# Ones matmuls ahead of the first rows, squares behind each tile's split, and a later first load of down-projection weights, in a one-core two-layer encoder step

## The chip, the core and the metric

The kernel runs on one core of one Trainium2 chip. The metric is device microseconds (us) of the whole program; a lower time is better. The kernel before took 1649.12 us, the median of three runs (1648.03 to 1649.99 us). A profiled execution of it was recorded too; all rows below come from that one.

## The reference, cut to what matters

One step of a streaming encoder with two layers, on 512 prompt rows and 32 sample rows of width 1024, in fp32. The start of the program, which the change touches, computes the first of these lines for layer 0:

```python
def rmsnorm(x, g):
    y = xf * lax.rsqrt(jnp.mean(xf * xf, axis=-1, keepdims=True) + EPS)
    return y * g
...
for l in range(DEPTH):                       # DEPTH = 2
    h = rmsnorm(x, w['norm_mix_g'])
    z = h @ w['w_in']                        # q, k, v, gmlp u and v: 1024 -> 2560
    ...                                      # differential attention, spatial gate, norms
    x = x + jnp.concatenate([o, g_out], -1) @ w['w_out']
    x = x + cross_attend(rmsnorm(x, w['norm_x_g']), mem_k, mem_v, wq_c, wo_c, xq_norm_g)
    g, up = jnp.split(rmsnorm(x, w['norm_ffn_g']) @ w['w_up'], 2, -1)   # 1024 -> 2 x 2816
    x = x + (silu(conv3(g)) * up) @ w['w_down']                         # 2816 -> 1024
```

Outputs are the rows after both layers and the new keys, values and convolution states.

## The kernel before, in words

Every large product is done with split operands: an fp32 tile is cut into a high part (a cast to fp32r by ScalarE, written ACT in the rows) and a low part (source minus high part, by VectorE, DVE), and three products (high by high, high by low, low by high) are summed in PSUM by TensorE (PE). Weights go through the same split: `emit_item` takes a loaded tile `raw` and makes the pair `hl` (L192 on ACT, L193 on DVE).

**Start (L1136 to L1186).** The gain row `mrow` and the 32 sample rows `xs` are loaded from ACT's queue. The first of four prompt tiles `xin` (128 rows by 1024, 512 KB each) is issued on SyncE's queue (SP); then `prefetch(4)` lets `load` issue weight loads, then the other three prompt tiles follow on the same queue. PE transposes each prompt tile in two halves of four 128 by 128 blocks (`pxin`, L1174) and the sample rows by 16 thin matmuls (`pxis`, L1179). `take` follows each: DVE multiplies by the gain into `xg` (L1162), ACT casts the high part into `hx` (L1163) and copies the plain rows into `x` (L1164), DVE makes the low part (L1165). After the loop over tiles, ACT squares the five row tiles (L1184), summing each row into one column of `sx`, from which `x_stats` makes the reciprocal roots (`rsq`), their diagonal matrices `dg` and the broadcast `rbc`. Since the mean is applied after the product, the first projection (`pr`, L370 to L372, 128 by 256 outputs) needs `hx` and `hl` and not the squares.

**Weight loads.** `load` keeps two tiles of kind "raw" (512 KB) and two of kind "rawb" (halves of a down-projection block, 384 KB) in flight. A tile is issued as soon as the tile two places ahead of it in its kind has been split. `items` is the list of all splits in order of use, `state["emitted"]` how many have been written out. The first "rawb" pair is used by item 74 in layer 0 and by item 266 in layer 1; in the kernel before it is issued at item 0, and at items 185 and 188.

**Order.** The instructions of each engine and queue run in the order in which a planner put them when the program was built: it walks the program with estimated durations and takes, among what it holds to be ready, the instruction that comes first in the text. So a change of the text can change the order of instructions in other places too.

Of the kernel before, what the change touches and what calls it, by code (L numbers as in the profile page):

```python
# [12 lines left out]
AF = mybir.ActivationFunctionType  # L13
ALU = mybir.AluOpType
# [5 lines left out]
SS = 32  # L20
# [16 lines left out]
def encoder_step(ctx: ExitStack, tc: tile.TileContext, a, o):  # L37
    nc = tc.nc
    vec, act, pool, pe, sp = nc.vector, nc.scalar, nc.gpsimd, nc.tensor, nc.sync
# [7 lines left out]
    def psR(name):  # L47
        return pp.tile([128, 512], F32, tag="R", bufs=4, name=name)

    def psS(name):  # L50
        return pp.tile([128, 512], F32, tag="S", bufs=2, name=name)
# [6 lines left out]
    def G(tag, shape, name, dt=F32):  # L58
        return gp.tile(shape, dt, tag=tag, bufs=GB[tag], name=name)

    def tmp(shape, name, tag="t", bufs=5, dt=F32):
        return tp.tile(shape, dt, tag=tag, bufs=bufs, name=name)

    ONCE = ("sx", "vx", "ve", "rx", "dgs", "ssm", "vm", "gss", "mss", "sss", "ls")

    def tiny(shape, name, dt=F32):
        return tp.tile(shape, dt, tag="y_" + name, bufs=1 if name in ONCE else 2, name=name)

# [6 lines left out]
    ones = cp.tile([128, 128], F32, name="ones")  # L75
# [10 lines left out]
    raws, items = [], []  # L86
# [4 lines left out]
    for i in range(NP):  # L91
        q = i // PART - 1
        n = min(PART, NP - PART * (q + 1)) * 4 - 1
        for b in range(4):
            PLAN.append(("gguu"[b], i, b % 2))
            p = 4 * (i - PART * (q + 1)) + b - 1
# [3 lines left out]
    def build_units():  # L100
        def ks(src, k0, n):
            return src[k0 * 128:(k0 + n) * 128].rearrange("(k p) c -> p k c", p=128)

        def item(tag, what, ids, n):
            items.append((tag, what, ids, n))
            for r in ids:
                raws[r][2] = len(items) - 1

        def raw(loads, nk, cols, kind="raw"):
            raws.append([loads, nk, None, cols, kind])  # L110
            return len(raws) - 1

        def two(tag, mat, cols):
            for k0 in (0, 4):
                c0, loads = 0, []
                for c, n in cols:
                    loads.append((0, 4, c0, n, ks(mat[:, c:c + n], k0, 4)))
                    c0 += n
                item(tag, None, (raw(loads, 4, 256),), 4)

        for l in range(DEPTH):
            wi = a["w_in"][l]
            kq = lambda h: two(f"kq{h}", wi, [(512 + 128 * h, 128), (128 * h, 128)])
            v_ = lambda j: two(f"v{j}", wi, [(1024 + 256 * j, 256)])
            u_ = lambda j: two(f"u{j}", wi, [(1536 + 256 * j, 256)])
            gv = lambda j: two(f"gv{j}", wi, [(2048 + 256 * j, 256)])
            for f, i in ((kq, 0), (v_, 0), (kq, 1), (kq, 2), (v_, 1), (kq, 3), (gv, 0), (u_, 0), (gv, 1), (u_, 1)):
                f(i)
            for j in range(4):
                src = a["w_out"][l][:, 256 * j:256 * j + 256].rearrange("(b q k p) c -> q b p k c", b=2, q=2, p=128)  # L130
                for q in range(2):
                    item(f"wout{j}", None, (raw([(2 * b, 2, 0, 256, src[q, b]) for b in range(2)], 4, 256),), 4)
            for h in range(4):
                for nm in ("wq", "wk") if h == 0 else ("wk", "wq"):
                    two(f"{nm}{h}", a[nm + "_c"][l], [(256 * h, 256)])
                two(f"wv{h}", a["wv_c"][l], [(256 * h, 256)])
            for j in range(4):
                two(f"wo{j}", a["wo_c"][l], [(256 * j, 256)])

            ids = None  # L140
            for what, i, j in PLAN:
                if what != "d":
                    c0 = 256 * i + 128 * j + (FF if what == "u" else 0)
                    item(f"{what}{i}_{j}", None, (raw([(0, 8, 0, 128, ks(a["w_up"][l][:, c0:c0 + 128], 0, 8))], 8, 128),), 8)
                    continue
                jj, m = j // 7, j % 7
                if m == 0:
                    src = a["w_down"][l][256 * PART * i:256 * PART * (i + 1), 256 * jj:256 * jj + 256].rearrange(
                        "(k e p) c -> e p k c", e=2, p=128)
                    ids = [raw([(0, PART, 0, 256, src[e])], PART, 256, "rawb") for e in range(2)]  # L150
                item(f"d{i}_{jj}", SEVEN[m], ids, PART)
                raws[ids[0]][2] = min(raws[ids[0]][2], len(items) - 1 - max(0, m - 3))
            for j in range(4):
                n = NF - 2 * PART * NB
                item(f"dp{j}", None, (raw([(0, n, 0, 256, ks(a["w_down"][l][:, 256 * j:256 * j + 256], NF - n, n))], n, 256),), n)
# [4 lines left out]
    state = {"emitted": 0, "popped": 0, "held": 0}  # L160
    SLOTS = 8
    RAWS = {"raw": 2, "rawb": 2}
    waiting, loaded = {}, {}

    def load():
        if not waiting:
            for kind in RAWS:
                waiting[kind] = [r for r in range(len(raws)) if raws[r][4] == kind]
                loaded[kind] = 0
        for kind, n in RAWS.items():  # L170
            while loaded[kind] < len(waiting[kind]):
                k = loaded[kind]
                if k >= n and raws[waiting[kind][k - n]][2] >= state["emitted"]:
                    break
                r = waiting[kind][k]
                loads, nk, _, cols, _ = raws[r]
                t = wp.tile([128, 1024 if kind == "raw" else 256 * PART], F32, tag=kind, bufs=n, name="raw")
                rv = t[:, 0:nk * cols].rearrange("p (k c) -> p k c", c=cols)
                for k0, kn, c0, cn, src in loads:
                    sp.dma_start(out=rv[:, k0:k0 + kn, c0:c0 + cn], in_=src)  # L180
                raw_t[r] = rv
                loaded[kind] += 1
# [39 lines left out]
    def prefetch(slots=SLOTS):  # L222
        while state["emitted"] < len(items) and state["held"] + cost(state["emitted"]) <= slots:
            state["held"] += cost(state["emitted"])
            emit_item()
# [76 lines left out]
    def psR2(name, n=0):  # L302
        f = psS if n % 3 == 2 else psR
        return [f(name + "a"), f(name + "b")]
# [832 lines left out]
    build_units()  # L1137
    mrow = tmp([8, 128], "mrow")
    act.dma_start(out=mrow, in_=a["norm_mix_g"][0].rearrange("(k p) -> k p", p=128))
    xs = G("zr", [128, 1024], "xins")  # L1140
    vec.memset(xs[32:64], 0.0)
    vec.memset(xs[64:128], 0.0)
    act.dma_start(out=xs[0:32], in_=a["x_sample"][0])
    xin = []
# [12 lines left out]
    def take(ps, k0, nk, t0, n):  # L1157

        ps = ps[:, 0:nk * n].rearrange("p (k t) -> p k t", k=nk)
        xg = tmp([128, 512], "xg")[:, 0:nk * n].rearrange("p (k t) -> p k t", k=nk)  # L1160
        h = [hx[:, k0:k0 + nk, j, t0:t0 + n] for j in range(2)]
        vec.tensor_tensor(out=xg, in0=ps, in1=gmix[:, k0:k0 + nk].unsqueeze(2).to_broadcast([128, nk, n]), op=ALU.mult)  # L1162
        act.copy(h[0], xg)  # L1163
        act.copy(x[:, k0:k0 + nk, t0:t0 + n], ps)  # L1164
        vec.tensor_tensor(out=h[1], in0=xg, in1=f32(h[0]), op=ALU.subtract)  # L1165

    sx = tiny([128, 5], "sx")
    pool.memset(sx, 1.0)
    for t in range(4):
        for hk in range(2):  # L1170
            ps = (psB if hk else psS)("pxin")
            for k in range(4):
                kt = 4 * hk + k
                pe.transpose(ps[:, 128 * k:128 * k + 128], xin[t][:, 128 * kt:128 * kt + 128], ident)  # L1174
            take(ps, 4 * hk, 4, 128 * t, 128)
        if t == 0:
            ps = psS("pxis")
            for kt in range(8):
                pe.matmul(out=ps[:, 32 * kt:32 * kt + 32], lhsT=xs[:, 128 * kt:128 * kt + 128], rhs=ident[:, 0:32],  # L1179
                          start=True, stop=True)  # L1180
            take(ps, 0, 8, S0, SS)
    for t, (v, n) in enumerate([(v, 128) for v in xin] + [(xs, SS)]):
        jk = G("t4", [128, 1024], "jk")
        act.activation(out=jk[0:n], in_=v[0:n], func=AF.Square, accum_out=sx[0:n, t:t + 1])  # L1184
    prefetch()
    sp.dma_start(out=rope, in_=a["rope"])  # L1186

# [1 line left out]
    for l in range(DEPTH):  # L1189
# [3 lines left out]
        r, ve, rbc = x_stats(True, sx if l == 0 else None)  # L1193
# [38 lines left out]
        for j in range(4):  # L1232
            w2 = pop(f"wout{j}")
            for i in range(2):
                ps = psR2("pwo", 2 * j + i + 2)
# [3 lines left out]
        mt, rm, vm = do_memT(l)  # L1239
        _, ve, _ = x_stats(False)  # L1240
        co = []
        for h in range(4):
# [7 lines left out]
            for dc in range(2):  # L1250
                t = G(COTAGS[2 * h + dc], [128, 2, T], "co", F32R)
                co.append(t)
            do_cross_out(l, h, mv, pT, pTs, co)
        for j in range(4):
            w2 = pop(f"wo{j}")
            for i in range(2):
                ps = psR2("pwc")
# [3 lines left out]
        _, _, rbc = x_stats(True)  # L1261
# [50 lines left out]
```

## Time and profile before

| | |
|---|---|
| median of three runs | 1649.12 us (1648.03 to 1649.99) |
| profiled execution, whole | 1648.65 us |
| its span, first to last instruction | 1646.6 us |
| PE busy | 1619.5 us, 98% of the span |
| DVE busy | 1149.7 us, 70% |
| ACT busy | 778.6 us, 47% |
| POOL (GpSimd) busy | 536.2 us, 33% |
| mean transfer rate over the span | 96 GB/s |

The span is what the profile shows; the execution is 2.05 us longer than it. Busy shares are means over the whole program. The start of the program, some 30 us, is told by the timelines below and not by these shares. In the timelines an x8 stands for eight instructions merged into one line, whose time is from the first's start to the last's end. A matmul with fp32 operands is two instructions; a transpose, and a matmul with fp32r operands, is one.

### The profile page before, as it was taken

The page shows a single profiled execution, that of the slowest core. Times are in us where ns is not written, and L with a number is a line of the kernel's source. Part 1 is how long each engine was busy: PE and PEld are TensorE (multiplying, and loading weights), DVE is VectorE, ACT ScalarE, POOL GpSimd, SP SyncE. Part 2 cuts the span into 40 slices and gives each one's busy share as a digit, 9 for nine tenths or more (in the row PEclk, how much of TensorE's full clock was granted, in tenths as well). Part 3 has the DMA queues.
Part 4 walks back from the last instruction along what each step waited for, and adds up shares of the span by engine and source line. Part 5 has one row for each costly group of instructions (what it writes and reads, how often), then busy time and mean ns, then how long its engine had stood idle before and what let it go on. Part 6 is the DMA issues. An engine that isn't in the chain of part 4 may idle for free.

```text
span 1646.6 us, 33007 instructions
## 1 busy us (share of the span) xinstructions
PE 1619.5 (98%) x12897; PEld 1591.7 (97%) x12897; DVE 1149.7 (70%) x2453; ACT 778.6 (47%) x1625; POOL 536.2 (33%) x910
## 2 busy tenths in 40 slices
PE   8999999999999999999999999999999999999998
PEld 8999999899999999999999999999999999999998
DVE  7778765655477777877768777655555777778774
ACT  6657744554344334343445685545543433343332
POOL 2110042222244654543321000422222545555440
PEclk9999999999999999999999999999999999999999
DMA  7322224332322332323342212243422323323322
GB/s 215 96 80 81 86 83 142 106 119 91 90 78 74 91 106 81 103 75 97 111 123 63 90 55 91 90 129 109 135 84 78 90 81 91 95 82 93 91 81 82
DMA packets 217633, 158.06 MB, mean 96 GB/s; under 512 B 8414, under 2 KB 216166, under 8 KB 217478
## 3 DMA queue, kind: packets, MB, share of 16 engines
q1 hardware_dynamic: 217414, 155.82, 31.2%
q8 instruction: 101, 1.65, 0.4%
q14 instruction: 54, 0.44, 0.1%
q10 hardware_dynamic: 64, 0.14, 0.0%
HBM read 144.83 MB, written 11.10 MB: 95 GB/s over the span
## 4 chain that ended last, share of the span: by engine, by line
PE 93%; DVE 2%; ACT 2%; POOL 2%; issue 1%; DMA 1%; ACTq 0%; SPq 0%; DVEq 0%; POOLq 0%
PE pfga L353 8%; PE pfgb L353 8%; PE pfua L353 8%; PE pfub L353 8%; PE p7a L1084 6%; PE pr L370 4%; PE pr L372 4%; PE pr L371 4%; PE p7c L1084 3%; PE pwoa L353 3%; PE pwca L353 3%; PE pqb L353 3%; PE pwob L353 3%; PE pqa L353 3%; PE pwcb L353 3%; PE pm L372 2%
## 5 line engine op out<-in xcount | busy, mean ns | idle before, releaser
L193 DVE TENSOR_TENSOR hl<-raw,hl 128x1024 fp32r<-128x1024 f32 x216 | 279.7, 1296 | 93.8 <-ACT hl L192 89.5
L192 ACT CAST hl<-raw 128x1024 fp32r<-128x1024 f32 x216 | 226.6, 1049 | 164.4 <-PE pm L371 37.5
L353 PE MATMUL pfga<-hx,hl 128*128 128x272 f32 x1056 | 264.5, 287 | 0.0
L353 PE MATMUL pfgb<-hx,hl 128*128 128x272 f32 x1056 | 264.4, 287 | 0.0
L353 PE MATMUL pfua<-hx,hl 128*128 128x272 f32 x1056 | 259.9, 288 | 3.0 <-DVE gb L1024 3.0
L353 PE MATMUL pfub<-hx,hl 128*128 128x272 f32 x1056 | 259.7, 287 | 0.0
L353 PEld LDWEIGHTS pfua<-hx,hl 128*128 128x128 f32 x1056 | 195.6, 188 | 3.2 <-DVE gb L1024 3.2
L353 PEld LDWEIGHTS pfga<-hx,hl 128*128 128x128 f32 x1056 | 198.5, 188 | 0.0
L353 PEld LDWEIGHTS pfgb<-hx,hl 128*128 128x128 f32 x1056 | 198.4, 188 | 0.0
L353 PEld LDWEIGHTS pfub<-hx,hl 128*128 128x128 f32 x1056 | 195.5, 188 | 0.0
L370 PE MATMUL pr<-hl,hx 128*128 128x256 f32 x512 | 145.6, 285 | 0.7 <-DVE zvs L413 0.7
L371 PE MATMUL pr<-hl,hx 128*128 128x256 f32 x512 | 146.0, 286 | 0.0
L372 PE MATMUL pr<-hl,hx 128*128 128x256 f32 x512 | 145.5, 285 | 0.0
L1084 PE MATMUL p7a<-at,hl 128*128 128x272 f32 x864 | 121.8, 287 | 0.0
L1084 PEld LDWEIGHTS p7a<-at,hl 128*128 128x128 f32 x864 | 113.3, 188 | 0.0
L210 ACT CAST hl<-S 128x384 fp32r<-128x384 f32 x96 | 48.4, 512 | 113.0 <-POOL S L200 40.9
L370 PEld LDWEIGHTS pr<-hl,hx 128*128 128x128 f32 x512 | 98.2, 192 | 1.4 <-DVE zvs L413 1.2
L372 PEld LDWEIGHTS pr<-hl,hx 128*128 128x128 f32 x512 | 97.0, 190 | 0.4
L371 PEld LDWEIGHTS pr<-hl,hx 128*128 128x128 f32 x512 | 97.1, 190 | 0.3
L210 ACT CAST hl<-raw 128x384 fp32r<-128x384 f32 x72 | 36.6, 511 | 108.3 <-PE pfub L353 60.9
L353 PE MATMUL pwca<-co,hl 128*128 128x272 f32 x384 | 87.5, 289 | 0.0
L353 PE MATMUL pwcb<-co,hl 128*128 128x272 f32 x384 | 87.1, 288 | 0.0
(393 smaller groups left out, 4201.6 us busy)
## 6 DMA issues: line engine op xcount, KB each, us to landing
raw<-in_w_up_dram SPq DMA_DIRECT2D x88, 512.0 KB
raw<-in_w_down_dram SPq DMA_DIRECT2D x48, 384.0 KB
raw<-in_w_in_dram SPq DMA_DIRECT2D x24, 512.0 KB
raw<-in_w_in_dram SPq DMA_DIRECT2D x32, 256.0 KB
raw<-in_w_out_dram SPq DMA_DIRECT2D x32, 256.0 KB
raw<-in_wq_c_dram SPq DMA_DIRECT2D x16, 512.0 KB
raw<-in_wk_c_dram SPq DMA_DIRECT2D x16, 512.0 KB
raw<-in_wv_c_dram SPq DMA_DIRECT2D x16, 512.0 KB
```

Source lines behind the costliest of these rows:

```text
L192: act.copy(hi, src)
L193: vec.tensor_tensor(out=lo, in0=src, in1=f32(hi), op=ALU.subtract)
L210: act.copy(hl[:, 0], src)
L353: pe.matmul(out=ps[0 if n0 == 0 else 1][:, 0:nn], lhsT=hl[wpart][:, kk, col * 128:col * 128 + 128], rhs=mv[:, n0:n0 + nn], start=first and ...
L370: pe.matmul(out=out, lhsT=lh(k), rhs=hl[0][:, k % 4], start=(k == 0), stop=False)
L371: pe.matmul(out=out, lhsT=lh(k), rhs=hl[1][:, k % 4], start=False, stop=False)
L372: pe.matmul(out=out, lhsT=ll(k), rhs=hl[0][:, k % 4], start=False, stop=(k == k8 - 1))
L1084: pe.matmul(out=ps, lhsT=w[:, wpart, k], rhs=mv[:, part], start=fresh and k == 0 and wpart + part == 0, stop=k == PART - 1 and wpart == 1, ...
```

## The change

Four edits. (1) Twenty matmuls of `ones` by `ones` (fp32, 128 columns) into a PSUM tile that nothing reads stand ahead of the loop over prompt tiles, and one Square of a column of `ones` on ACT ahead of them. (2) The squares of a row tile come right after that tile's two `take`s, in two halves of 512 columns, each summed into its own column of `sx2`; their unused elementwise result goes over `xg`, which `take` now returns. DVE adds the two columns into `sx`. The tile of 32 sample rows comes last. (3) A "rawb" tile is issued only when its first item is at most 8 items ahead of the item that is written out (`EARLY`). (4) So at the start the two first "rawb" tiles are no longer issued ahead of the prompt tiles 1 to 3, but at item 66; layer 1's first pair is issued at item 258.

```diff
-    ONCE = (..., "mss", "sss", "ls")
+    ONCE = (..., "mss", "sss", "ls", "sx2")
...
-            raws.append([loads, nk, None, cols, kind])
+            raws.append([loads, nk, None, cols, kind, len(items)])
...
+    EARLY = 8
...
-                loads, nk, _, cols, _ = raws[r]
+                loads, nk, _, cols, _, first = raws[r]
+                if kind == "rawb" and first > state["emitted"] + EARLY:
+                    break
...
+    dum = tmp([128, 1], "dum", tag="aTs", bufs=1)
+    act.activation(out=dum, in_=ones[:, 0:1], func=AF.Square)
+    pw = psR("pwarm")
+    for i in range(20):
+        pe.matmul(out=pw[:, 0:128], lhsT=ones, rhs=ones, start=True, stop=True)
     xs = G("zr", [128, 1024], "xins")
...
         vec.tensor_tensor(out=h[1], in0=xg, in1=f32(h[0]), op=ALU.subtract)
-
-    sx = tiny([128, 5], "sx")
-    pool.memset(sx, 1.0)
+        return xg.rearrange("p k t -> p (k t)")
+
+    sx2 = tiny([128, 5, 2], "sx2")
+    pool.memset(sx2, 0.5)
+    def squares(t, hk, n, v, junk):
+        act.activation(out=junk[0:n], in_=v[0:n, 512 * hk:512 * hk + 512], func=AF.Square,
+                       accum_out=sx2[0:n, t, hk:hk + 1])
+    junks = []
     for t in range(4):
         for hk in range(2):
...
-            take(ps, 4 * hk, 4, 128 * t, 128)
+            junks.append(take(ps, 4 * hk, 4, 128 * t, 128))
+        for hk in range(2):
+            squares(t, hk, 128, xin[t], junks[2 * t + hk])
         if t == 0:
...
-    for t, (v, n) in enumerate([(v, 128) for v in xin] + [(xs, SS)]):
-        jk = G("t4", [128, 1024], "jk")
-        act.activation(out=jk[0:n], in_=v[0:n], func=AF.Square, accum_out=sx[0:n, t:t + 1])
+    for hk in range(2):
+        squares(4, hk, SS, xs, junks[7])
+    sx = tiny([128, 5], "sx")
+    vec.tensor_tensor(out=sx, in0=sx2[:, :, 0], in1=sx2[:, :, 1], op=ALU.add)
     prefetch()
```

## Rows read from the trace of the kernel before

**Rows 1.** The page: busy shares, and the chain that ended last, by engine.
```profile
PE 1619.5 (98%) x12897; PEld 1591.7 (97%) x12897; DVE 1149.7 (70%) x2453; ACT 778.6 (47%) x1625; POOL 536.2 (33%) x910
...
PE 93%; DVE 2%; ACT 2%; POOL 2%; issue 1%; DMA 1%; ACTq 0%; SPq 0%; DVEq 0%; POOLq 0%
```
**Rows 2.** PE's waits, whole span: releaser, us in total, times, longest.
```profile
PE pxin L1174 <- DMA xin<-in_x_prompt_dram: 4.9, 1, 4.9
PE po L654 <- ACT e L651: 3.8, 5, 1.5
PE pfua L353 <- DVE gb L1024: 3.0, 2, 1.5
```
**Rows 3.** Timeline of PE from 4.5 us: start, us, engine, line, operation.
```profile
4.89 0.87 PE L1174 MATMUL pxin<-ident,xin 128*128 128x128 f32 x3 [4.89 <-DMA xin<-in_x_prompt_dram]
5.89 1.33 PE L1174 MATMUL pxin<-ident,xin 128*128 128x128 f32 x5
7.01 3.46 PE L1179 MATMUL pxis<-ident,xins 128*128 128x32 f32 x16
10.29 0.56 PE L370 MATMUL pr<-hl,hx 128*128 128x256 f32 x1
...
13.21 1.91 PE L1174 MATMUL pxin<-ident,xin 128*128 128x128 f32 x8
...
15.34 0.41 PE L370 MATMUL pr<-hl,hx 128*128 128x256 f32 x1
15.55 0.34 PE L371 MATMUL pr<-hl,hx 128*128 128x256 f32 x1
15.73 0.28 PE L372 MATMUL pr<-hl,hx 128*128 128x256 f32 x1
15.85 0.28 PE L370 MATMUL pr<-hl,hx 128*128 128x256 f32 x1
```
**Rows 4.** Stretches from the start: busy us by engine, granted clock, DMA share, GB/s.
```profile
0.00:9.40 9.40, 4.51 (x21) 4.19 (x22) 4.69 (x8) 4.56 (x7) 4.59 (x23) 1.00 0.85 233
```
**Rows 5.** Timeline of PE, later.
```profile
16.55 1.03 PE L1174 MATMUL pxin<-ident,xin 128*128 128x128 f32 x8
...
29.05 0.28 PE L372 MATMUL pr<-hl,hx 128*128 128x256 f32 x1
```
**Rows 6.** Timeline of DVE, start of the program.
```profile
0.90 0.17 DVE L76 MEMSET ones<- 128x128 f32 x1 [0.90 <-PEq L1299]
...
6.41 0.69 DVE L1162 TENSOR_TENSOR xg<-pxin,gmix 128x512 f32<-128x512 f32 x1 [0.24 <-PE pxin L1174]
...
8.25 1.23 DVE L193 TENSOR_TENSOR hl<-raw,hl 128x1024 fp32r<-128x1024 f32 x1 [0.29 <-ACT hl L192]
...
24.14 1.23 DVE L193 TENSOR_TENSOR hl<-raw,hl 128x1024 fp32r<-128x1024 f32 x1
```
**Rows 7.** Timeline of ACT, start of the program.
```profile
4.83 1.28 ACT L1184 ACT_TABLE_LOAD   x1 [4.83 <-DMA xin<-in_x_prompt_dram]
6.12 1.06 ACT L1184 ACTIVATE jk<-xin 128x1024 f32<-128x1024 f32 x1
...
7.18 1.04 ACT L192 CAST hl<-raw 128x1024 fp32r<-128x1024 f32 x1
8.12 0.61 ACT L1163 CAST hx<-xg 128x512 fp32r<-128x512 f32 x1
8.64 0.58 ACT L1164 COPY x<-pxin 128x512 f32<-128x512 f32 x1
...
12.41 1.06 ACT L1184 ACTIVATE jk<-xin 128x1024 f32<-128x1024 f32 x1 [0.67 <-DMA xin<-in_x_prompt_dram]
```
**Rows 8.** Timeline of SP's queue: issues, x of them merged.
```profile
1.26 2.08 SPq L180 DMA_DIRECT2D raw<-in_w_in_dram  x4
3.38 2.43 SPq L180 DMA_DIRECT2D raw<-in_w_down_dram  x2
5.86 1.56 SPq L1147 DMA_DIRECT2D xin<-in_x_prompt_dram  x3
```

More of the change, by code (lines that the diff above doesn't have):

```diff
@@ L62, in tmp @@
         return tp.tile(shape, dt, tag=tag, bufs=bufs, name=name)
-    ONCE = ("sx", "vx", "ve", "rx", "dgs", "ssm", "vm", "gss", "mss", "sss", "ls")
+    ONCE = ("sx", "vx", "ve", "rx", "dgs", "ssm", "vm", "gss", "mss", "sss", "ls", "sx2")
     def tiny(shape, name, dt=F32):
```

## The prediction

> **What bounds the kernel now.** I read the page first. PE is busy 98% of the span and holds 93% of the chain that ended last; no other engine holds more than 2% of it [rows 1]. So a saving counts only if PE's work starts earlier, runs faster or waits less. Next I read PE's waits. The longest is the first, 4.9 us for the first prompt rows; the fourteen other kinds come to some 18 us over the whole program, are waits on DVE and ACT of at most 1.5 us each, and none is for a weight transfer [rows 2]. The change therefore can't win by feeding weights sooner. It can win in the first 16 us, and the timeline of PE shows how. [...] Eight transposes take 1.91 us before the switch and 1.03 us after it [rows 3, 5]; less the last one's own time of about 0.41 and 0.28 us that is a pitch of 0.214 and 0.107 us.
>
> **The sum that can be won.** Between 4.89 and 15.73 us (10.84 us) PE did 16 transposes, one small transpose of the gains, 16 thin instructions and 17 `pr` matmuls. At the upper rate that is 17 x 0.107 + 16 x 0.107 + 17 x 0.12 = 5.6 us. (The thin ones ran at 3.46 us for 16, as slow as full transposes [rows 3], so I price them as such.) 5.2 us are lost to the lower rate and 4.9 us to the wait for rows. The transfer itself is not made faster: the first prompt tile is first in its queue before and after, so the 4.9 us stay.
>
> **The ones matmuls.** Twenty fp32 matmuls are 40 instructions. They need only `ones`, written at 0.90 + 0.17 = 1.07 us [rows 6]; I let them start at 1.2 us. They stand ahead of the transposes in the text, so I take it that the planner puts all 40 in front, and PE runs in order. At 0.214 us each all 40 would take 8.6 us and end at 9.8 us; at 0.107 us, 4.3 us and 5.5 us. Either way they end after the rows are there at 4.89 us: the first transpose is late by 0.6 to 4.9 us, and this is the price of the edit. In return what follows runs at the upper rate. Where between the ends? The nearest row is the stretch of dense `pr` matmuls: it began at 10.29 and the rate rose at about 15.6, 5.3 us later, with eight transposes inside it [rows 3]. Taken over, the rate rises at 1.2 + 5.3 = 6.5 us, after 25 instructions; the other 15 take 1.6 us, and the ones end at 8.1 us. Counted from PE's first work instead (10.7 us after 4.89), it would not rise within them. I take 8.1 us. Then the 5.6 us of work end at 13.7 us instead of 15.73: a gain of 2.0 us.
>
> [...] After the rise in this trace the rate held through eight transposes in a row at 16.55 us [rows 5]. [...]
>
> **The first tile's chain.** With PE late, DVE and ACT idle until 8.1 us and then come in series: four transposes (0.6 us), `xg` 0.69 us [rows 6], the cast 0.61 us [rows 7], together 1.9 us, to about 10.0. PE has the other transposes and the thin matmuls to do until 8.1 + 0.43 + 0.43 + 1.7 = 10.7 us, so the chain is covered by 0.7 us. The cover goes if DVE is given the second weight split (1.23 us [rows 6]) ahead of `xg`: its weights are there at about 8 us (the first prompt tile, the sample rows and 1.05 MB of weights are 1.7 MB; 233 GB/s held over the first 9.4 us [rows 4]), so it could end at 10.0 and `pr` would begin at 11.5, 0.8 us late. Between 0 and 0.8 I take 0.2, since today's order puts both `xg` ahead of it. The table load of 1.28 us and the first square of 1.06 us, which stood on ACT between the rows' arrival and the casts [rows 7], both leave that place: the one is done while the rows travel, the other goes behind the casts. On the path they bring nothing, since PE's thin matmuls ended after the casts anyway.
>
> **The squares.** Five squares of 1.06 us become ten halves. A 512-column ACT operation follows the next after 0.52 us (8.12 to 8.64 [rows 7]), plus about 0.1 for reading the sum: ten by 0.62 is 6.2 against 5.3 us, 0.9 us more on ACT, plus one tiny DVE addition. Nothing of it is on PE. What hides it: ACT's work from the first cast on is eight casts and eight copies (8 us), the sample's pair (0.7), ten halves (6.2) and two weight casts (1.9), 16.8 us, so it ends at 9.4 + 16.8 = 26.2 us if it never idles. The next projection begins at 29.1 us now [rows 5] and would at 27.1; its first weight low part would be made by about 27.4 at worst, against 24.14 + 1.23 us for the same work of its second pair now [rows 6]. So the cover shrinks from some 5 us to about nothing at the worst, and I take 0 with a bound of 0.5 us lost. The sums come later (about 25 us instead of 18), and `rsq`, `dg` and the broadcast with them; the planner sees that and may place their matmuls later. Bound: 1 us of waiting, taken 0.
>
> **The transfers.** Two issues of 384 KB leave SP's queue ahead of the prompt tiles 1 to 3 [rows 8]. Those tiles' rows land later than 4.9 us; ACT waited for tile 1 until 12.41 us [rows 7], PE came to it only at 13.21 [rows 3]. At the stretch's rate 0.79 MB are some 3 us, so tile 1 lands at about 9.5. PE would come to it at 10.7 at the earliest: hidden, but without this edit (landing at 12.4) an earlier PE could have waited for it up to 1.7 us. The edit thus guards the gain rather than adding to it. The issue at item 66, eight items ahead of use, costs nothing: an item of the FFN is 48 matmuls, some 6 us of PE, and no PE wait is for weights [rows 2]. The same holds for layer 1's pair.
>
> **Sum.** 2.0 - 0.2 = 1.8 us off the profiled execution of 1648.65 us: 1646.8 us. That execution is 0.5 us under the median of 1649.12. A difference under 0.2% (3.3 us) is about what a measurement of this kernel can't tell from no change, and the forecast falls under it.
>
> **Rivals.** (a) *The rate rises early*, within the first third of the ones. At the limit, all at the upper rate, they end at 5.5 us and the gain is 15.73 - 5.5 - 5.6 = 4.6 us: 1644.0. For it: they are dense and of one kind. Against: no row shows a rise sooner than 5.3 us after dense work began; a gain over 3.3 needs the ones to end by 6.8 us, so a rise by 3.7 us. Waits of PE elsewhere (18 us) could also shrink by a new order. Chance 0.2. (b) *The gain is absorbed*: PE arrives earlier and waits for `hx`, `hl` or the broadcast (the bounds of 0.8, 0.5 and 1 us). 1647.9 to 1649.5. For it: ACT's and DVE's cover goes to nothing by my own sum; against: none of these is above 1 us. Chance 0.14. (c) *The rate falls back* ahead of `pr` and rises as late as it did behind the first dense work: half of 5.3 us is lost, 1646.8 + 2.65 = 1649.5. [...] Chance 0.06. (d) *Slower*: the ones don't lift the rate. Then they hold PE until 9.8 us and all that follows runs as today, 4.9 us later: 1653.6. It decides from here: if the rate has not risen by about 10.7 us, the ones cost more than they give. For it: 5.4 us of transposes and thin fp32 matmuls did not lift it [rows 3]. Against: what stood right before the rise was dense work of one kind, as the ones are. A worse order in a later stage would also land here. Chance 0.1. (e) The forecast, a gain of 0.7 to 3.3 us: chance 0.5.
>
> **How the numbers follow.** 1646.8 is (e)'s. The range takes in (a), (b), (c) and (e), with 0.1 to 0.9 us at the ends for the runs' own spread, and leaves out (d): 1643.9 to 1650.4. Faster by over 0.2%: (a) and a little of (e), 0.22. Slower by over 0.2%: most of (d), 0.09. Within: 0.69.
>
> **What would show it.** In the new profile: 40 `pwarm` instructions ending near 8 us with the pitch falling from 0.21 to 0.11 us among them; the first transpose right behind them; thin matmuls at 0.11 us; the first `pr` near 10.9 us with a pitch of 0.12 us; prompt tile 1 ready before PE asks; PE's first projection ending near 27 us with no wait above 0.5 us in it. The prediction is wrong if the planner does not put the ones first, if the pitch falls much sooner or only after 10 us, or if PE's waits past 30 us change by more than 1.5 us in sum.

## The result, and the profile after

The kernel after takes 1658.08 us, the median of six runs (1657.19 to 1659.44), against 1649.05 us of the kernel before (six runs, 1648.03 to 1649.99). The ratio is 1.0054, with a 95% interval of 1.0043 to 1.0065: slower by 9.0 us, where 1.8 us faster was forecast. Its profiled execution took 1659.11 us, with a span of 1657.4 us.

The page of the kernel after, busy shares and chain by engine, hardly differs from [rows 1]: PE's busy time is 5.8 us more, though it now holds 7.4 us of ones, which fill what had been the wait for the first rows; the rest of the longer span is idle time of PE.

```profile
PE 1625.3 (98%) x12937; PEld 1597.4 (96%) x12937; DVE 1151.3 (69%) x2454; ACT 779.6 (47%) x1636; POOL 536.4 (32%) x910
...
PE 93%; DVE 2%; ACT 2%; DMA 1%; POOL 1%; issue 0%; SPq 0%; ACTq 0%
```

PE's waits in the kernel after. The 4.9 us for the first prompt rows [rows 2] is gone, as the ones now fill it. At the top stands a wait that the kernel before did not have: 7.7 us in one piece, for the operands `z` and `zvs` of the first attention transposes (`ptr`). A second new one, 1.9 us for constants (`prow`), is fourth.

```profile
PE ptr L556 <- DVE zvs L519: 7.7, 1, 7.7
...
PE po L657 <- ACT e L654: 2.4, 4, 1.5
PE prow L445 <- DMA srow<-in_state_ffn_conv_dram: 1.9, 1, 1.9
```

The start, timeline of PE in the kernel after, against [rows 3]:

```profile
1.12 7.37 PE L1148 MATMUL pwarm<-ones 128*128 128x128 f32 x40 [1.12 <-DVE ones L76]
...
8.57 1.09 PE L1190 MATMUL pxin<-ident,xin 128*128 128x128 f32 x8
9.50 1.87 PE L1197 MATMUL pxis<-ident,xins 128*128 128x32 f32 x16
...
11.60 0.36 PE L373 MATMUL pr<-hl,hx 128*128 128x256 f32 x1
11.80 0.28 PE L374 MATMUL pr<-hl,hx 128*128 128x256 f32 x1
...
20.38 2.06 PE L390 MATMUL prs<-hl,xsm 128*64 128x256 f32 x16
```

The ones alone, from two windows of the timeline (2 to 6 us and 7 to 8 us; an instruction that reaches into the window is counted):

```profile
1.71 4.69 PE L1148 MATMUL pwarm<-ones 128*128 128x128 f32 x21
...
6.76 1.50 PE L1148 MATMUL pwarm<-ones 128*128 128x128 f32 x12
```

Less the last one's own time (0.42 and 0.28 us), the first line is 20 steps of 0.213 us and the second 11 of 0.111 us. The rate rose at about 6.7 us, after 26 of the forty. The granted clock reads 1.00 before the rise all the same (the ones from 5 to 6 us: busy us, instructions that touch the stretch, granted clock, DMA share, GB/s):

```profile
5.00:6.00 1.00, 1.00 (x7) 1.00 1.08 267
```

So the start went nearly as forecast: the ones end at 8.49 us, the transposes and thin matmuls behind them run at the upper rate (1.09 us for eight, where eight behind the rise in [rows 5] took 1.03), and the sample rows' product `prs` starts at 20.38 us instead of 21.47, 1.1 us ahead. Then it is lost. Windows of the kernel after, and behind them the same of the kernel before (busy us by engine, granted clock, DMA share, GB/s):

```profile
30.00:45.00 15.00, 13.11 (x98) 12.75 (x96) 9.36 (x38) 5.75 (x15) 2.62 (x6) 0.89 0.51 140
45.00:60.00 15.00, 7.27 (x50) 7.04 (x49) 11.13 (x27) 6.17 (x13) 1.22 (x2) 0.77 0.43 135
```

```profile
30.00:45.00 15.00, 15.00 (x127) 14.70 (x126) 11.66 (x36) 6.19 (x13) 2.13 (x5) 1.00 0.49 137
45.00:60.00 15.00, 14.66 (x123) 14.36 (x122) 8.16 (x21) 7.70 (x20) 1.74 (x4) 1.00 0.44 136
```

Between 30 and 60 us PE is busy 9.3 us less than before, and in these stretches the granted clock is 0.89 and 0.77. The timeline of PE shows both waits and what follows each, and the line behind it the same `ptr` in the kernel before, without a wait:

```profile
30.70 0.28 PE L374 MATMUL pr<-hl,hx 128*128 128x256 f32 x1
32.87 0.30 PE L445 MATMUL prow<-ident,rows 124*128 124x124 f32 x1 [1.89 <-DMA srow<-in_state_ffn_conv_dram]
...
33.76 0.42 PE L373 MATMUL pr<-hl,hx 128*128 128x256 f32 x1
...
37.38 0.29 PE L375 MATMUL pr<-hl,hx 128*128 128x256 f32 x1
...
54.54 1.94 PE L556 MATMUL ptr<-ident,z 128*128 128x128 f32 x8 [7.73 <-DVE zvs L519]
...
56.56 0.56 PE L373 MATMUL pr<-hl,hx 128*128 128x256 f32 x1
...
57.94 0.28 PE L373 MATMUL pr<-hl,hx 128*128 128x256 f32 x1
```

```profile
44.25 1.04 PE L553 MATMUL ptr<-ident,z 128*128 128x128 f32 x8
```

From 33.76 to 37.38 us the pitch is 3.62 / 17 = 0.213 us instead of 0.12: 1.6 us lost. Eight `ptr` take 1.94 us instead of 1.04 (0.9 more), and what follows up to 57.94 loses about 0.7 more. The sum is 7.7 + 1.9 + 3.2 - 1.1 (the lead of the start) = 11.7 us. The first `pua` (the product behind layer 0's attention) starts at 150.57 us, 11.6 us later than before (138.95). Later PE's waits for `e` are 2.4 us instead of 3.8 [rows 2]. 11.6 - 1.4 = 10.2, and the profiled execution is 1659.11 - 1648.65 = 10.5 us longer. The whole loss is there by the first `pua`, and the sum finds it in the first 60 us.

The terms of this sum don't count alike. The wait for the constants and the slow stretch behind it (1.9 and 1.6 us) lie ahead of the wait for `z`: without them PE would have come to `ptr` earlier and, with `z` no earlier, waited longer there. What sets the loss is that `ptr` starts at 54.54 us instead of 44.25 and that the rate is low behind it: 10.3 + 1.6 us, against 11.6 at the first `pua`. The experiments bear this out: e2 has no wait for the constants, e7 one of 0.3 us, and they lose 8.8 and 8.6 us.

Why `z` is late, timeline of DVE in the kernel after (`sx` is the sum of squares, `rx` the last step of the reciprocal root, `lp` the product of the lambda rows, `ss` the squares' sum of k and q, the last `zvs` the end of `z`):

```profile
33.20 0.29 DVE L447 COPY cols<-prow 128x124 f32<-128x124 f32 x1 [2.30 <-PE prow L445]
34.46 0.29 DVE L473 TENSOR_TENSOR lp<-lv 128x128 f32<-128x128 f32 x1 [0.96 <-DMA lv<-in_lambda_k_dram]
...
36.17 0.15 DVE L1203 TENSOR_TENSOR sx<-sx 128x5 f32<-128x5 f32 x1
...
39.43 0.17 DVE L333 COPY rx<-rxy 128x5 f32<-128x5 f32 x1
...
42.49 1.22 DVE L534 TENSOR_REDUCE ss<-sq 128x16 f32<-128x1024 f32 x1 [1.82 <-ACT sq L528]
...
46.87 1.23 DVE L196 TENSOR_TENSOR hl<-raw,hl 128x1024 fp32r<-128x1024 f32 x1 [1.02 <-ACT hl L195]
...
48.43 1.20 DVE L196 TENSOR_TENSOR hl<-raw,hl 128x1024 fp32r<-128x1024 f32 x1
...
54.32 0.21 DVE L519 TENSOR_TENSOR zvs<-skq 32x64 f32<-32x64 f32 x1
```

And of ACT:

```profile
31.72 0.62 ACT L1181 ACTIVATE xg<-xins 32x512 f32<-32x512 f32 x1
32.25 0.19 ACT L1181 ACTIVATION_READ_ACCUMULATOR xg<-xins 32x1 f32 x1
...
39.70 0.48 ACT L586 ACTIVATE vr<-pr,rx 128x256 f32<-128x256 f32 x1 [4.35 <-DVE rx L333]
...
41.36 1.09 ACT L528 ACTIVATE sq<-pr 128x512 f32<-128x512 f32 x2
```

The same places in the kernel before, DVE and then ACT:

```profile
27.38 0.15 DVE L330 COPY rx<-rxy 128x5 f32<-128x5 f32 x1
...
35.59 1.21 DVE L531 TENSOR_REDUCE ss<-sq 128x16 f32<-128x1024 f32 x1
...
44.01 0.20 DVE L516 TENSOR_TENSOR zvs<-skq 32x64 f32<-32x64 f32 x1
44.46 1.23 DVE L193 TENSOR_TENSOR hl<-raw,hl 128x1024 fp32r<-128x1024 f32 x1 [0.25 <-ACT hl L192]
```

```profile
18.04 0.19 ACT L1184 ACTIVATION_READ_ACCUMULATOR jk<-xins 32x1 f32 x1
...
31.86 0.60 ACT L525 ACTIVATE sq<-pr 128x512 f32<-128x512 f32 x1
```

Read together they give three links. First, the squares, written over `xg`, must wait until DVE has made the low part from it, and stand behind casts on ACT: the last ends at 32.4 us. In the kernel before the last ended at 18.2 us, and `rx` started at 27.38. Second, in the order of DVE's timeline the columns' copy `cols` (33.20 us), `lp` (34.46, after 0.96 us idle for the lambda rows) and a weight split (35.03) stand ahead of `sx` (36.17). Third, in the order of ACT's, `sq` (41.36), which needs no root, stands behind `vr` (39.70), which waits 4.35 us for `rx`. Before, `sq` ran at 26.97 and 31.86 us. So `z` ends 10.3 us later (its last operation starts at 54.32 instead of 44.01).

Of these 10.3 us, 6.9 are there when DVE sums `sq` (42.49 instead of 35.59). The other 3.4 come behind it: two weight splits (46.87, after a wait of 1.02 us for the weight's high part, and 48.43) stand on DVE inside the chain from `ss` to the end of `z`, where in the kernel before they come behind its end (44.46 and 46.15). The runs below show the same: both splits stand inside `z` in e2, e3, e7, e10 and e14, which lose most, one of them in e8, e9 and e13, none in e1, e4 and e5. No run changes this place by itself, so its share of the loss is read from the timelines only.

SP's queue, against [rows 8]: prompt tiles 1 to 3 moved up as forecast, but the down-projection pair is issued at 11.41 us and not at item 66. The place in the text moved to item 66. That the planner, which takes what is ready, brought the issue forward is a reading of how it works; no run tests it.

```profile
3.39 2.20 SPq L1156 DMA_DIRECT2D xin<-in_x_prompt_dram  x3
...
11.41 1.69 SPq L183 DMA_DIRECT2D raw<-in_w_down_dram  x2
```

### The profile page after: what moved, and what is told of

It reads as the page before. It is cut to its first block, busy times and chain, and to the rows that moved or that the text cites. A ratio compares the mean times of both kernels' runs of the same rounds, so it can differ in the third digit from the quotient of the medians.

```text
span 1657.4 us, 33104 instructions
## 1 busy us (share of the span) xinstructions
PE 1625.3 (98%) x12937; PEld 1597.4 (96%) x12937; DVE 1151.3 (69%) x2454; ACT 779.6 (47%) x1636; POOL 536.4 (32%) x910
## 4 chain that ended last, share of the span: by engine, by line
PE 93%; DVE 2%; ACT 2%; DMA 1%; POOL 1%; issue 0%; SPq 0%; ACTq 0%
PE pfua L356 8%; PE pfga L356 8%; PE pfub L356 8%; PE pfgb L356 8%; PE p7a L1087 7%; PE pr L373 3%; PE pr L374 3%; PE pr L375 3%; PE p7c L1087 3%; PE pwca L356 3%; PE pwob L356 3%; PE pqb L356 3%; PE pwoa L356 3%; PE pqa L356 3%; PE pwcb L356 3%; PE pm L375 2%
```

## The experiments

"z" is the start of the last operation of `z` (before: 44.01; after: 54.32), "ptr" PE's wait in front of the first attention transposes, both in us from the profile. A later `z` costs only where PE is at `ptr` before it: in e1 and e5 PE comes there later itself and does not wait. The ratio is to the kernel before, run on the same chip.

| run | time, us | ratio (95%) | z | ptr |
|---|---|---|---|---|
| after | 1658.08 | 1.0054 (1.0043 to 1.0065) | 54.32 | 7.7 |
| e1 without the squares' edit | 1648.69 | 1.0005 (0.9995 to 1.0014) | 45.86 | none |
| e2 squares' edit alone | 1657.13 | 1.0052 (1.0036 to 1.0069) | 50.95 | 6.2 |
| e3 `dg` in another tag | 1653.79 | 1.0033 (1.0021 to 1.0045) | 49.55 | 6.0 |
| e4 squares in their own buffer | 1648.1 | 0.9998 (0.9988 to 1.0007) | 45.14 | 0.2 |
| e5 ones alone | 1647.28 | 0.9995 (0.9985 to 1.0005) | 47.08 | none |
| e6 later load alone | 1647.8 | 0.9999 (0.9989 to 1.0008) | 42.34 | none |
| e7 sample's squares first | 1656.68 | 1.0050 (1.0034 to 1.0066) | 51.36 | 7.2 |
| e8 = e7 + e3 | 1651.7 | 1.0019 (1.0009 to 1.0028) | 47.60 | 4.2 |
| e9 = e8 + lambda rows early | 1651.45 | 1.0022 (1.0012 to 1.0031) | 48.66 | 2.1 |
| e10 = after + lambda rows early | 1655.84 | 1.0045 (1.0030 to 1.0060) | 51.32 | 6.2 |
| e11 = e1 + lambda rows early | 1650.47 | 1.0012 (1.0003 to 1.0022) | 45.92 | none |
| e12 = e4 + lambda rows early | 1651.4 | 1.0019 (1.0009 to 1.0029) | 45.08 | none |
| e13 = e8 + lambda work on GpSimd | 1648.18 | 1.0004 (0.9995 to 1.0014) | 45.30 | 1.8 |
| e14 = after + lambda work on GpSimd | 1654.93 | 1.0038 (1.0023 to 1.0053) | 51.41 | 7.2 |
| e15 = e1 + lambda work on GpSimd | 1648.42 | 1.0001 (0.9992 to 1.0011) | 42.81 | none |
| e16 = e4 + lambda work on GpSimd | 1649.02 | 1.0005 (0.9996 to 1.0015) | 42.71 | none |

**e1, e2, e5, e6: which part.** e1 is the kernel after with the lines of the squares put back; the other three are the kernel before with one part of the change.

> Ones matmuls and the later first load of down-projection weights are kept, the squares are put back as before (whole tiles, after the loop, result into a tile of their own). Theory A (the late sums of squares): the loss of 9 us goes and the gain of the start is left, 1646 to 1648 us, PE's wait for z (7.7 us) gone. Theory B (the ones matmuls take PE time and the rate falls later): nothing changes, 1656 to 1659. Theory C (down-projection weights now sit in the queue ahead of the constants' rows): 1654 to 1659, the wait for the constants (1.9 us) stays.

> Only the squares' edit on the kernel before. Theory A: it makes the loss by itself, 1656 to 1661 us, with a PE wait for z of 6 to 9 us near 50 us. Theories B and C: as before, 1648 to 1651.

> Only the ones matmuls and the early Square on the kernel before. Theory A (late sums are the whole loss): no loss, 1646 to 1649.5 us; the start gains 1 to 2 us on PE and loses most of it to waits for ACT and DVE, as with the squares put back (1648.7). Theory B: the ones cost, 1653 or more.

> Only the later first load of the down-projection weights on the kernel before. Theory A: 1647.5 to 1650 us, no difference, since PE is slow and busy until 15.6 us whatever the rows do; the two loads go behind the prompt tiles by a few issues and not to item 66. Theory C: 1653 or more, the constants late.

The squares' edit alone carries the loss (e2), and without it the rest is the same as before within 0.15% (e1). Ones and later load can't be told from no change, alone or together. e1 came out over its range (1648.69 against 1646 to 1648), since no gain of the start is left in it. In e1 PE starts `prs` at 21.66 us, against 20.38 in the kernel after and 21.47 before: the start's gain is there only with the squares behind the casts. e5 lacks the later load: PE then waits 0.9 us for prompt tile 1, runs at the lower rate until 18.3 us and starts `prs` at 23.52. Its time is still no longer, so the wait that this edit guards against is real, but the end does not tell of it. At the first `pua` e5's PE is 3.0 us behind the kernel before, at the end of the span 0.9; where it gets 2 us back was not followed. e5's ten times spread from 1646.39 to 1649.31 us, five of them under the lowest of the kernel before beside them (1647.55), and the profile is of the one at 1649.2; whether the ones alone gain something is open.

**e3, e4: what in the squares' edit.**

```diff
-        dg = G("t4", [128, 4, 128], "dg")                         # e3
+        dg = G("t4" if sx is None else "e", [128, 4, 128], "dg")
...
-            squares(t, hk, 128, xin[t], junks[2 * t + hk])        # e4
+            squares(t, hk, 128, xin[t], G("e", [128, 512], "jk"))
...
```

> The changed kernel, with the diagonal matrices dg of the first x_stats in tag e in place of t4, so that the squares sq of the first projection need not follow dg in one tag; sums of squares stay late. Theory A in its narrow form (the late sums hold sq back through the shared tag, and ACT's queue puts vr, which waits for the reciprocal root, ahead of sq): PE's wait for z of 7.7 us falls to under 2.5, 1650 to 1653 us; the wait for the constants of 1.9 us stays. If the late reciprocal root holds z back by itself: z can't be scaled ahead of 39.5 us, but needs some 5 us after it, so 1655 or more. Theories B and C: 1657 to 1659.

> The changed kernel, but the unused results of the squares go to tiles of tag e and not over xg, so a square waits for the rows alone and xg's buffers come free as before. Theory A: the sums are there near 20 us again, no wait for z and none for the constants, 1646 to 1649 us. If the cost lies in halving and moving the squares as such: 1653 or more. Theories B and C: 1656 to 1659.

With a buffer that nothing else holds, the squares run as soon as their rows land, `sx` is there at 21.69 us, and the loss is gone: it does not lie in halves instead of wholes or in two sums. In e3 `sq` runs again at 24.73 and 31.58 us, ahead of `vr`; so what had put it behind `vr` was the tag that `dg` and `sq` share. That takes 3.5 of the 9.0 us away, as `z` ends 4.8 us earlier; the time falls between the run's two ranges, and the wait of `ptr` (6.0 us) is far over the 2.5 that were expected. The rest stays because `sx` now starts at 38.28 us, behind `lp`, and `z` needs both; and the two weight splits still stand inside `z` (45.53 and 47.75 us). The wait for the constants, which was expected to stay, is gone in e3; it lay ahead of the wait for `z`, and `sx` comes no earlier without it, so it does not account for the gain.

**e7, e8: earlier sums.** The squares of the 32 sample rows, the last to end, move up behind the first tile's; e8 adds e3's edit.

```diff
         if t == 0:
...
+            for hk in range(2):
+                squares(4, hk, SS, xs, junks[hk])
...
-    for hk in range(2):
-        squares(4, hk, SS, xs, junks[7])
```

> The changed kernel with one move: the two half squares of the 32 sample rows stand right behind the first tile's and not behind the last one's. Theory A: the last of the ten sums comes at about 28 us and not at 32, DVE adds them ahead of the constants' work, the reciprocal root is there at about 33 and not at 39.4 us, PE's wait for z falls from 7.7 us to under 2.5: 1648 to 1652 us. If it is the squares of the prompt tiles that hold all up, or the place of any square is of no weight: 1656 or more.

> As the run before, and dg in tag e, so that sq does not follow it. Theory A: PE's wait for z under 1 us, the start's gain of 1 us over the kernel before left on PE: 1645 to 1648.5 us. If the gain of the start is eaten by other waits all the same: 1648.5 to 1650.

e7 missed: `sx` starts at 28.66 us instead of 36.17, and the time is nearly the same. Sums that come 7.5 us earlier therefore do not help by themselves. DVE's timeline in e7 shows what took their place: the chain of the root (`rxt`, `rxy`) is cut in two by `lp`, which was placed in the middle of it and waits 3.36 us for the lambda rows.

```profile
31.91 0.15 DVE L254 TENSOR_TENSOR rxt<-rxy 128x5 f32<-128x5 f32 x1
35.42 0.29 DVE L473 TENSOR_TENSOR lp<-lv 128x128 f32<-128x128 f32 x1 [3.36 <-DMA lv<-in_lambda_k_dram]
35.63 1.22 DVE L196 TENSOR_TENSOR hl<-raw,hl 128x1024 fp32r<-128x1024 f32 x1
...
36.94 0.16 DVE L255 TENSOR_TENSOR rxt<-rxt,rxh 128x5 f32<-128x5 f32 x1
...
38.64 0.17 DVE L333 COPY rx<-rxy 128x5 f32<-128x5 f32 x1
```

The kernel before has this wait too (`lp` at 33.94 us, after 2.73 us idle), but there the root was done at 27.5. e8 missed too (1651.7 us against 1645 to 1648.5). It has the same picture, with `lp` waiting 2.90 us in the middle of the root.

**e9 to e12: the lambda rows loaded early.** The four rows are loaded from ACT's queue beside the sample rows, into a free buffer.

```diff
     act.dma_start(out=xs[0:32], in_=a["x_sample"][0])
+    LV[0] = lambdas(G("p", [128, 4, 64], "lv"), 0, act)
...
```

> The kernel of e8 (squares of the sample rows early, dg in a tag of its own) with the layer's four lambda rows loaded from ScalarE's queue beside the sample rows, into a tag that is still free, instead of late from SP's queue. Theory A (in e7 and e8 the root chain on VectorE was held for about 3 us by the product lp of the lambda rows, which stood in front of it and waited for their transfer): lp's wait of 2.9 us is gone, rx ends at 33 to 36 us instead of 39.64, the wait of ptr for zvs falls from 4.2 to under 1.5 us, and the time to 1646 to 1649.5. Theory B (the squares' place on ScalarE and the two further weight splits ahead of z hold z, not lp): rx moves, but z still ends later than 46.5 us, ptr waits over 2.5 us, and the time stays at 1650.5 to 1652.5.

> The changed kernel as it is, with the four lambda rows loaded early as in e9 and nothing else. Theory A (three links in a row: the squares end late at about 32 us, then lp in front of the sum, then sq behind dg and vr): only lp's link goes, about 3 us: rx ends at 35 to 37 us instead of 39.43, the wait of ptr for zvs falls from 7.7 to 4 to 6 us, and the time to 1653 to 1656. Theory B (the late squares and the buffers alone decide): rx and the time as in the changed kernel, 1657 to 1659. Theory C (lp's wait alone decides): ptr waits under 1.5 us and the time is 1647 to 1650.

> Control for e9 and e10: the ones and the held-back down-projection load with the squares as they were before (the kernel of e1, 1648.69), and the lambda rows loaded early. Theory A (lp costs only where the sums come behind it, and there they came ahead of it): the time stays within 1 us of e1's, 1647.5 to 1649.7. Theory B (the early load gives something by itself, by freeing a buffer of tag t or by lp's own wait): 1645 to 1647.3; then what e9 and e10 gain isn't all the root chain's.

> The kernel of e4 (the squares' results into a buffer of their own instead of over xg; 1648.1) with the lambda rows loaded early. Theory A: with the sums done by 22 us nothing is left that waits behind lp, so the time stays within 1 us of e4's, 1647 to 1649. Theory B (the early sums together with a VectorE queue free of lp's wait let z end ahead of the kernel before): z ends before 43 us instead of 45.2 and the time is 1645 to 1646.8, faster than both kernels.

These did not settle it. The controls became slower (e11 by 1.8 us against e1, e12 by 3.3 against e4), both out of their ranges: with the added transfers PE waits at prompt tile 1 (in e9, e10 and e12 for its rows, in e11 for a weight split) and then runs at the lower rate, as its timeline in e9 shows (four transposes in 1.09 us, where the kernel after takes 0.6; eight in 1.91):

```profile
12.17 1.09 PE L1196 MATMUL pxin<-ident,xin 128*128 128x128 f32 x4 [1.82 <-DMA xin<-in_x_prompt_dram]
...
13.49 1.91 PE L1196 MATMUL pxin<-ident,xin 128*128 128x128 f32 x8
```

In e9 `lp` waits no more and ptr's wait halves, but `rx` starts at 40.15 us, not at 33 to 36, and the time is that of e8. e10's time fell into theory A's range (its wait of `ptr`, 6.2 us, just over it), but its gain of some 2 us over the kernel after is as large as what the controls lose, so its size can't be read.

**e13 to e16: the lambda work off DVE.** Its transfer stays where it was; product, sum (by halving), difference and the eye block go to GpSimd.

```diff
-        vec.tensor_tensor(out=lp, in0=lv[:, 0:4:2], in1=lv[:, 1:4:2], op=ALU.mult)
+        pool.tensor_tensor(out=lp, in0=lv[:, 0:4:2], in1=lv[:, 1:4:2], op=ALU.mult)
+        for w in (32, 16, 8, 4, 2, 1):
+            pool.tensor_tensor(out=lp[:, :, 0:w], in0=lp[:, :, 0:w], in1=lp[:, :, w:2 * w], op=ALU.add)
...
-        vec.tensor_reduce(out=ls, in_=lp, axis=AX, op=ALU.add)
+        pool.tensor_copy(ls, lp[:, :, 0])
...
```

> The kernel of e8 with the whole of the lambda work (product, sum, difference and the eye block) on GpSimd instead of VectorE; its transfer stays where it was, so the start isn't touched as in e9. Theory A (lp's wait of 2.90 us inside VectorE's queue is what was left of e8's loss): rx ends at 36 to 37 us instead of 39.64, z at 44 to 46 instead of 47.7, the wait of ptr for zvs is under 2 us instead of 4.2, and the time 1647 to 1649.5, the same as before within 0.1%. Theory B (something else of the squares' edit holds z): ptr still waits over 3 us and the time stays at 1650.5 to 1652.5.

> The changed kernel with the lambda work on GpSimd and nothing else. Theory A (three links; lp's is only the 1.5 us that it idles and works in the changed kernel, since the sums end at 32.25 us and the columns' copy holds VectorE to 33.5 anyway): rx ends at 37.5 to 38.5 us instead of 39.43, ptr waits 5.5 to 7 us instead of 7.7, and the time is 1655 to 1657.5. Theory C (lp's wait is the cause by itself): ptr waits under 2 us and the time is 1647 to 1650.

> Control: the kernel of e1 (ones and held-back load, squares as before; 1648.69) with the lambda work on GpSimd. Theory A (there the root chain ends at 26.44 us, ahead of lp, so lp's wait costs nothing): 1647.7 to 1649.7. Theory B (the move gives something by itself): under 1647.5, and e13 and e14 are to be read less that gain.

> The kernel of e4 (squares' results in a buffer of their own; 1648.1) with the lambda work on GpSimd. Theory A: nothing on the path is behind lp, so 1647.1 to 1649.1. Theory B (z ends ahead of the kernel before and PE loses no time at ptr): 1645.5 to 1647, faster than both kernels.

e13 answers: the same halves over the same `xg`, and no measurable loss. DVE's timeline in e13 has the root chain, the sums of k and q and both splits without an idle between them:

```profile
29.07 0.17 DVE L1205 TENSOR_TENSOR sx<-sx 128x5 f32<-128x5 f32 x1 [0.76 <-ACT xg L1183]
...
31.90 1.21 DVE L536 TENSOR_REDUCE ss<-sq 128x16 f32<-128x1024 f32 x1
...
35.92 0.21 DVE L333 COPY rx<-rxy 128x5 f32<-128x5 f32 x1
```

and PE's, a wait of 1.76 us with the upper rate held behind it (1.06 us for eight transposes):

```profile
45.20 1.06 PE L558 MATMUL ptr<-ident,z 128*128 128x128 f32 x8 [1.76 <-DVE z L521]
```

The controls e15 and e16 stay within 1 us of e1 and e4, so the move gives nothing by itself. From e8 to e13 the medians fall by 3.5 us and the ratios by 0.0015 (2.5 us), with intervals that overlap; PE's wait for `z` falls by 2.4 us, and the low rate behind it is gone. The move took `lp`'s wait of 2.90 us out of DVE's queue, but also DVE's other lambda work, so that the wait alone is worth all of it is likely and not shown. In e14 the other links are still there, and 6.9 of the 9.0 us remain. It came out just under its range (1654.93 against 1655 to 1657.5): `rx` starts at 36.73 instead of 39.43, but ACT's exponential of the lambda sums now waits for GpSimd until 38.86 us and holds `vr` and `sq` behind it.

No version measurably beat the kernel before: e5, the lowest, is at 0.9995 with an interval that holds 1.

## Why the prediction was wrong, step by step

**The ones and the rate: right.** End 8.49 us (forecast 8.1), rise at about 6.7 us after 26 instructions (6.5 after 25), a pitch of 0.213 us before it and 0.111 us after it (0.214 and 0.107), the work behind them at the upper rate. That the rise came so close is in part luck: in the other runs with the same ones, all started at 1.1 us, the forty took 6.34 us (e9) to 7.63 us (e13), and by the two pitches, an estimate, the rise came after 16 to 29 of them. Rival (a) did not happen, and rival (d)'s mechanism, ones that don't lift the rate, did not either: its sign came true through another cause, the worse order in a later stage that it named in half a sentence without a price.

**The transposes behind the ones.** They did not let the rate fall: they ran at the upper rate themselves (1.09 us for eight), and `pr` began at 11.60 us and had the pitch of 0.12 us that the sum took (12.97 to 13.09), so rival (c) failed in the kernel after. In e5 the same transposes and thin matmuls, at the upper rate too (1.10 us for eight, 1.87 for the 16 thin ones), are followed by waits of 0.58 and 0.94 us, and behind the second the pitch is 0.21 us until 18.3. No run separates the stretch from the waits, so a fall by transposes alone, as rival (c) prices it, was not shown.

**The first tile's chain: right.** PE is not idle between the ones and 12.5 us, and then waits 0.23 us for a low part; 0.2 was taken. The first `pr` starts at 11.60 us instead of 10.9: the ones end 0.4 us later than forecast, and four transposes of tile 1 come ahead of it, another 0.4. The gain at `prs` is 1.1 us instead of 1.8: the mechanism was right, the size too large.

**The squares on ACT: right in themselves.** No PE wait of the first projection is due to them, and e4 shows that ten halves cost nothing that can be measured.

**The late sums: the step that failed.** The prediction said "The sums come later (about 25 us instead of 18), and `rsq`, `dg` and the broadcast with them; the planner sees that and may place their matmuls later. Bound: 1 us of waiting, taken 0." The last square ended at 32.4 us and DVE added the sums at 36.17. I had not asked what each square waits for: by writing over `xg` it waits for DVE's low part, and so it was ordered behind work that my sum left out. ACT did run densely, with 1.4 us idle from its first cast (10.40 us, not 9.4) to the last square; but four weight casts and not two, and four small operations of the next step, stand ahead of that square, which together makes about 32.4 us out of 26.2. And I followed the sums to the broadcast only. Their dearer consumer is `z`: its norm needs `ve`, made from the sums, and `sq` stands behind `vr` and so behind `rx`. PE waited 7.7 us for `z`, not 1, and lost 3.2 us more at the lower rate behind its two new waits. The prediction's own last sign of being wrong, PE's waits past 30 us changing by more than 1.5 us, is what happened. e4 shows that writing the squares over `xg` is necessary for the loss: with a buffer of their own they are early again and the loss is gone. e13 shows that it is not enough: the sums are still late there (29.07 us against 21.69 in e4). Short of e4, no single link takes the loss away: undoing one (e3, e7, e14) leaves 5.5 to 8.6 us, undoing two (e8) 3.6, easing all three (e13) none that can be measured. In e7, e8 and e13 the first link is only eased, as DVE adds the sums some 7 us earlier than in the kernel after, and in e4 14.

**The transfers: place wrong, price right.** Issued at 11.41 us and not at item 66; e6 shows no effect.

**What stays open.** The wait of 1.9 us for `prow`: its rows share buffers with the squares' `xg`, which the squares hold longer. But e2, e3, e8 and e13 write over `xg` too and have no such wait (e7 and e14 have 0.3 and 0.6 us), so something else has a part in it that I did not separate.

## What to carry to other kernels

When a small operation moves later, follow its result to every consumer, and in each engine's queue look at what will then stand in front of it: the dearest was not the nearest consumer, but one two links on, behind a product waiting for a late transfer and, once late, behind weight splits that used to follow it. Writing an unused result over a buffer that was still read was not free here: DVE added the sums at 36.17 us, against 21.69 with a buffer of their own (e4), and `sq` came behind `vr`; the free buffer removed the loss (e4, ratio 0.9998). The gain of 1.1 us at the start was worth nothing here, as a later wait of 7.7 us absorbed it.

## What the runs showed of the hardware that was not expected

The rate of PE fell behind quite short waits, and not always. After 1.9 us idle (30.98 to 32.87 in the kernel after, behind 10 us of dense matmuls) `pr` ran first at 0.12 us and from 33.76 at 0.213, with a granted clock of 0.58 between 34 and 38 us. After 1.76 us idle in e13 it did not fall: eight transposes took 1.06 us, `pr` had a pitch of 0.12 us behind them, and the granted clock was 1.00 between 44 and 48 us. After 1.82 us idle in e9 it was low at once (1.09 us for four transposes, against 0.60 in the kernel after). The ones started at 1.1 us in every run that has them, but the rate rose anywhere from 4.5 us (e9) to 7.2 us (e13), an estimate from the time of the forty (6.34 and 7.63 us) and the two pitches. The column of the granted clock says 1.00 for the first us of the ones, whose pitch is 0.213 us there and 0.111 later: at the start of this program the pitch is the witness. Sixteen thin fp32 matmuls of 32 columns took 1.87 us at the upper rate, each about as long as a transpose of 128 columns (1.09 us for eight).
